# Depthwise convolution taps of a conformer/retention trunk: ScalarE's products summed by accumulating transfers, fewer taps on TensorE, a new order of the planned stage

## The chip, the cores and the metric

The program runs on one core of a Trainium2 chip. The metric is the device time of one execution in microseconds; lower is better. All arithmetic keeps float32 accuracy: a float32 operand of a large matrix product is split into a high part of type float32r and a low part (the rest), and three products (high times high, high times low, low times high) are added in PSUM.

## The reference

Two layers on a sequence of 1024 positions with 1024 channels. Layer 0 mixes with a convolution module, layer 1 with retention; a squared-ReLU MLP follows each. Only layer 0's front part is touched here.

```
cond = silu(c)
for i in range(2):
    mod = cond @ ada_w[i] + ada_b[i]
    sh1, sc1, g1, sh2, sc2, g2 = split(mod, 6)
    h = rmsnorm(x, norm_mix_g[i]) * (1 + sc1) + sh1
    if i == 0:                                   # conformer_conv
        a, g = split(h @ w_pw1 + b_pw1, 2)
        u = a * sigmoid(g)
        u = depthwise_conv(u, w_dw, width=31, causal) + b_dw
        u = layernorm(u) * ln_g + ln_b
        y = silu(u) @ w_pw2 + b_pw2
    else:
        y = retention(h, ...)
    x = x + g1 * y
    h = rmsnorm(x, norm_mlp_g[i]) * (1 + sc2) + sh2
    x = x + g2 * (square(relu(h @ mlp_w1[i])) @ mlp_w2[i])
return rmsnorm(x, final_norm_g)
```

## The kernel before, in words

Channels lie on the 128 partitions (8 tiles, index j or kt), positions along the free dimension in two halves of 512 (t = 0 and t = 1). `layer_conv` builds layer 0's convolution module for both halves and seven eighths of the MLP for half 0 as a list of operations; a planner (`Plan`) then puts them in order. It is a list scheduler: it holds a time for each engine (P TensorE, V VectorE, A ScalarE, G GpSimd, D the SyncE queue of loads), a duration for each operation and a table of priorities `PR`, and picks the operation that can begin first, ties by priority. What it emits is a fixed program order for each engine. On the chip each engine goes through its own list in that order and stops at a semaphore that isn't there yet, so an instruction that waits holds up all behind it on its engine. Everything after `layer_conv` (rest of the MLP, retention, the second MLP, the final norm) is written out by hand and is not touched.

The planned stage does this. SyncE loads half 0 of x, the 16 tiles of `ada` that give shift and scale (sixteen dot products, `moddot`: one pass of a 128x1024 tile times the silu'd condition with a sum, by VectorE alone, or by GpSimd's multiply and ScalarE's sum where `M0POOL`, `M1POOL` or `MODPOOL` say so). From them come `G` and `Sh`, one column of 8 each. Then h0 (8 pieces, split in high and low, tiles hA) is formed, and TensorE begins `pw1`: per channel tile j and half t, 16 steps of three products into two PSUM tiles. The first three channel tiles (`FIRST`) are begun piece by piece as h0 arrives. `pw1` gives u(j,t) (tile x0 or x1, 30 columns of halo ahead of 512).

The 31 taps of u(j,t) are divided by the tables `NPE` (taps on TensorE, a diagonal 128x128 matrix that ScalarE makes, one float32 product per tap, two matmul records each), `NPOOL` (taps whose product ScalarE makes, tile prod, and GpSimd adds to tile cacc) and the rest (VectorE, `acc = u*w + acc` on two PSUM accumulators in turn, so that neighbours do not depend on each other). Two VectorE additions then join cacc and the two accumulators and put the result back into u. When all eight u(j,0) are done, the layer norm (`ln`) gives z0 (tiles hA again), `pw2` multiplies it, a norm (`norm_mlp`) follows, and TensorE runs seven blocks of the MLP on half 0. Meanwhile VectorE, ScalarE and GpSimd do the taps of half 1, whose layer norm gives z1 (tiles hB) for the second `pw2`.

Weights come as 128x1024 float32 tiles (raw, a ring of two); ScalarE copies the high part and VectorE or, where `WPOOL` says so, GpSimd subtracts to get the low part (both into a ring of nine tiles, whl).

In the kernel before, the lines that matter are L263 to L265 (the three products), L625 (low part of a weight tile), L644 (low part of a piece of h0 or h1), L639 (low part of a piece of z), L657 and L654 (moddot on VectorE and on GpSimd), L760 and L763 (G and Sh), L823 (tap on TensorE), L835 (tap on VectorE), L840 and L843 (product on ScalarE and its addition on GpSimd), L845 and L846 (the two joining additions), and L501, a float32 accumulating transfer that GpSimd issues in the second MLP, far behind this stage.

Of the kernel before, what the change touches and what calls it, by code (L numbers as in the profile page):

```python
# [1437 lines left out]
```

## Time and profile before

| | |
|---|---|
| median of three runs | 2687.4 us (2685.89 to 2691.25) |
| the profiled execution's own time | 2684.62 us |
| its span in the trace | 2682.8 us |
| mean granted TensorE clock | 0.983 of full |
| TensorE busy | 2583.2 us (96%) |
| VectorE busy | 1771.8 us (66%) |
| ScalarE busy | 1167.7 us (44%) |
| GpSimd busy | 398.0 us (15%) |

Shares over the whole span mix stages with different limits. The planned stage is the first quarter: its last TensorE work stands at about 721 us, and in it VectorE and GpSimd are far busier than in the mean. TensorE is called busy from the start of the first of several overlapping products to the end of the last; so its rate is read from the distance between starts, not from the length of one record. The same holds for VectorE, whose records overlap by a tenth of a microsecond or so.

### The profile page before, as it was taken

Reading aid. Unit: us, or ns where it says so; the run is one execution under the profiler, and the core shown is the slowest. Engines: PE = TensorE matmul, PEld = TensorE weight load, DVE = VectorE, ACT = ScalarE, POOL = GpSimd, SP = SyncE. Lnnn points to the kernel's source line nnn. Section 1 sums busy time; section 2 is a strip of 40 time slices with the busy share of each in tenths; the row PEclk is TensorE's granted clock in tenths of the full one; section 3 lists DMA queues with packets and bytes.
Section 4 is the critical chain, followed back from the end, with each engine's and each line's share of the span. In section 5 each row is a group of like instructions: output and inputs, shape, how many; then the busy total and the mean of one; then the engine's idle time right before and its main releaser. Section 6 shows DMA issues by size and latency. Waiting matters only on the chain.

```text
span 2682.8 us, 29885 instructions
## 1 busy us (share of the span) xinstructions
PE 2583.2 (96%) x11306; PEld 2089.1 (78%) x11306; DVE 1771.8 (66%) x2513; ACT 1167.7 (44%) x1762; POOL 398.0 (15%) x308
## 2 busy tenths in 40 slices
PE   2999999999999999999999999999999999999996
PEld 1666777888787888788888888888887888888785
DVE  7799999966477445645555665365567677665636
ACT  4666866463222323343433633334545443444323
POOL 3677439100000000000000000000000122111202
PEclk6999999999999999999999999999999999999997
DMA  7622322242376333322233232232332565334712
GB/s 255 204 71 87 114 91 87 88 133 93 119 235 220 101 96 94 116 89 87 71 94 95 72 102 86 80 94 71 95 125 68 114 119 125 75 81 104 196 48 79
DMA packets 95635, 293.26 MB, mean 109 GB/s; under 512 B 10625, under 2 KB 13057, under 8 KB 95362
## 3 DMA queue, kind: packets, MB, share of 16 engines
q1 hardware_dynamic: 78848, 261.37, 30.4%
q0 software_dynamic: 13824, 25.17, 6.2%
q10 hardware_dynamic: 2818, 4.81, 0.5%
q8 instruction: 89, 1.46, 0.2%
q14 instruction: 56, 0.46, 0.1%
HBM read 255.65 MB, written 35.65 MB: 109 GB/s over the span
## 4 chain that ended last, share of the span: by engine, by line
PE 69%; issue 14%; DVE 7%; DMA 4%; POOL 3%; ACT 2%; DVEq 0%; ACTq 0%; POOLq 0%; SPq 0%
PE mm L264 20%; PE mm L263 20%; PE mm L265 20%; DMA araw<-ada 3%; POOL xd L501 3%; PE mm L1064 2%; PE mm L1066 2%; PE mm L1065 2%; DVE acc L835 1%; PE acc L823 1%; DVE araw L324 1%; DVE araw L657 1%; POOL cacc L843 1%; DVE whl L625 1%; PE ax L708 0%
## 5 line engine op out<-in xcount | busy, mean ns | idle before, releaser
L263 PE MATMUL mm<-hA,whl 128*128 128x512 f32 x1200 | 481.0, 401 | 42.3 <-ACT whl L624 39.4
L251 DVE TENSOR_TENSOR whl<-raw,whl 128x1024 fp32r<-128x1024 f32 x240 | 293.3, 1223 | 339.5 <-ACT whl L250 244.3
L250 ACT CAST whl<-raw 128x1024 fp32r<-128x1024 f32 x240 | 251.9, 1050 | 603.9 <-PE mm L264 206.7
L265 PE MATMUL mm<-hA,whl 128*128 128x512 f32 x1200 | 473.9, 395 | 5.7 <-DVE whl L625 3.6
L264 PE MATMUL mm<-hA,whl 128*128 128x512 f32 x1200 | 474.7, 396 | 2.4 <-DVE hA L644 2.2
L263 PE MATMUL mm<-hid,whl 128*128 128x512 f32 (+1 forms) x976 | 375.2, 385 | 4.3 <-ACT hid L286 3.0
L264 PE MATMUL mm<-hid,whl 128*128 128x512 f32 (+1 forms) x976 | 373.5, 384 | 1.2 <-DVE hid L287 1.2
L265 PE MATMUL mm<-hid,whl 128*128 128x512 f32 (+1 forms) x976 | 372.5, 383 | 0.0
L501 POOL DMA_DIRECT2D xd<-ev x72 | 64.2, 913 | 1879.5 <-DVE ev L497 1877.5
L263 PEld LDWEIGHTS mm<-hA,whl 128*128 128x128 f32 x1200 | 226.9, 189 | 99.9 <-ACT whl L624 42.0
L265 PEld LDWEIGHTS mm<-hA,whl 128*128 128x128 f32 x1200 | 226.8, 189 | 60.9 <-DVE whl L625 7.1
L264 PEld LDWEIGHTS mm<-hA,whl 128*128 128x128 f32 x1200 | 226.8, 189 | 58.3 <-issue 4.8
L843 POOL TENSOR_TENSOR cacc<-cacc,prod 128x512 f32<-128x512 f32 x166 | 253.3, 1528 | 112.2 <-ACT prod L840 56.4
L263 PE MATMUL mm<-hB,whl 128*128 128x512 f32 x576 | 229.4, 398 | 0.0
L264 PE MATMUL mm<-hB,whl 128*128 128x512 f32 x576 | 225.0, 391 | 0.0
L265 PE MATMUL mm<-hB,whl 128*128 128x512 f32 x576 | 224.8, 390 | 0.0
L263 PEld LDWEIGHTS mm<-hid,whl 128*128 128x128 f32 x976 | 183.5, 188 | 46.0 <-ACT hid L286 8.6
L264 PEld LDWEIGHTS mm<-hid,whl 128*128 128x128 f32 x976 | 183.8, 188 | 39.4 <-DVE hid L287 3.1
L265 PEld LDWEIGHTS mm<-hid,whl 128*128 128x128 f32 x976 | 183.8, 188 | 35.6 <-issue 0.2
L835 DVE SCALAR_TENSOR_TENSOR acc<-x,vec,acc 128x512 f32<-128x512 f32 x239 | 166.8, 747 | 2.3 <-PE acc L823 1.4
L625 DVE TENSOR_TENSOR whl<-raw,whl 128x1024 fp32r<-128x1024 f32 x92 | 122.7, 1340 | 36.1 <-PE mm L264 10.9
L624 ACT CAST whl<-raw 128x1024 fp32r<-128x1024 f32 x92 | 95.8, 1045 | 101.2 <-DMA raw<-w 42.9
(270 smaller groups left out, 4337.7 us busy)
## 6 DMA issues: line engine op xcount, KB each, us to landing
raw<-w SPq DMA_DIRECT2D x192, 512.0 KB, 3.6
araw<-ada SPq DMA_DIRECT2D x80, 512.0 KB, 4.4
raw<-pw SPq DMA_DIRECT2D x38, 512.0 KB, 4.2
xd<-ev POOLq DMA_DIRECT2D x72, 256.0 KB, 6.2
raw<-rqk SPq DMA_DIRECT2D x32, 512.0 KB, 3.5
raw<-rv SPq DMA_DIRECT2D x32, 512.0 KB, 3.6
raw<-rgate SPq DMA_DIRECT2D x32, 512.0 KB, 3.5
raw<-rout SPq DMA_DIRECT2D x32, 512.0 KB, 3.5
```

Source lines behind the costliest of these rows:

```text
L250: nc.scalar.copy(hi[i], raw[:, i * W : i * W + W])
L251: nc.vector.tensor_tensor(lo[i], raw[:, i * W : i * W + W], hi[i].bitcast(F32), ALU.subtract)
L263: nc.tensor.matmul(out, whi, rhi, start=start, stop=False)
L264: nc.tensor.matmul(out, whi, rlo, start=False, stop=False)
L265: self.last_mm = nc.tensor.matmul(out, wlo, rhi, start=False, stop=stop)
L501: nc.gpsimd.dma_start(xd[n][t], e, accum_op=ALU.add)
L624: op("A", 0.95 / n, pa, lambda h=h, src=src: nc.scalar.copy(E[h], E[raw][:, src]), r=[raw], w=[h], a={h: (tag, kw)})
L625: op(low, dur / n, pa, lambda h=h, l=l, src=src: eng.tensor_tensor(E[l], E[raw][:, src], E[h].bitcast(F32), ALU.subtract), r=[raw, h], w=[ ...
L835: op("V", 0.68, p, lambda s=s, a=a: nc.vector.scalar_tensor_tensor(E[a], sl(s), wv(s), E[a], ALU.mult, ALU.add), r=[u], w=[a])
L843: op("G", 1.28, p, lambda pr=pr: nc.gpsimd.tensor_tensor(E[ca], E[ca], E[pr], ALU.add), r=[pr], w=[ca])
L1064: nc.tensor.matmul(vps[jt], hh[0], wh, start=kt == 0, stop=False)
L1065: nc.tensor.matmul(vps[jt], hh[0], wl, start=False, stop=False)
```

## The change

Taps. `NPE` falls from 53 taps in all to 10, `NPOOL` from 182 to 136, so VectorE's share goes from 261 to 350. GpSimd no longer adds: ScalarE's first product of each of two chains is written to a cacc tile (five in the ring, two before), and each further product is added to it by an accumulating transfer (SBUF to SBUF, 128x512 float32), which GpSimd issues. Each such transfer waits for the one ahead of it in its chain. VectorE's first tap of each accumulator reads cacc, the last tap writes into u, and one joining addition is left of two. The planner gets a field `late`: 5.0 us in which a transfer's result is not there after its issue.

Modulation at the beginning: no moddot of the first sixteen is on GpSimd any more (six were); `G` and `Sh` are formed by ScalarE instead of VectorE. Of the 32 later ones 24 are on GpSimd (10 before). Weights: the low part of every second tile of four of the five groups is made by GpSimd (39 tiles; none before). MLP: for one of four hidden tiles ScalarE does relu and square in PSUM, where VectorE multiplied. All priorities in `PR` are new.

```diff
-X1_AT = 70
-RINGS = dict(raw=2, tmp=4, araw=2, whl=9, hid0=4, sum=2, prod=4, cacc=2, dg=6)
+X1_AT = 80
+RINGS = dict(raw=2, tmp=4, araw=2, whl=9, hid0=4, sum=2, prod=4, cacc=5, dg=2)
...
-NPOOL = ((15, 13, 14, 3, 15, 9, 11, 11), (14, 13, 13, 12, 2, 11, 14, 12))
-NPE = ((6, 8, 6, 6, 1, 0, 6, 10), (6, 0, 0, 0, 0, 1, 3, 0))
+NPOOL = ((0, 7, 9, 6, 12, 6, 12, 8), (10, 23, 2, 5, 12, 11, 4, 9))
+NPE = ((0, 0, 5, 0, 0, 0, 0, 0), (0, 0, 0, 0, 4, 0, 1, 0))
+EVDMA = ()
+RELUA = (0,)
...
-WPOOL = dict(w0=0, w1=8, pw2=0, mlp=0, pw21=0)
-M0POOL = (1, 2, 3)
-M1POOL = (0, 4, 7)
-MODPOOL = dict(m2=2, m3=0, m4=2, m5=3)
+WPOOL = dict(w0=0, w1=2, pw2=2, mlp=2, pw21=2)
+M0POOL = ()
+M1POOL = ()
+MODPOOL = dict(m2=1, m3=0, m4=1, m5=1)
...
+            if o[9]:
+                free["D"] = max(free["D"], t) + 1.7
...
-            op("V", 0.13, ("G", kt), lambda kt=kt: nc.vector.scalar_tensor_tensor(
-                c1("G", kt), c1(("mod", 1), kt), adb[:, kt : kt + 1], self.v("mix_g", kt), ALU.add, ALU.mult),
+            op("A", 0.25, ("G", kt), lambda kt=kt: nc.scalar.activation(
+                c1("G", kt), c1(("mod", 1), kt), AF.Identity, scale=self.v("mix_g", kt), bias=adb[:, kt : kt + 1]),
...
+            fresh = {c for c in range(2) if c or not npe}
+            nca = len(fresh)
+            for i in range(npool):
+                s, c = TAPS - 1 - i, 1 - i % nca
+                ca = k("cacc", c)
+                pr = ca if i < nca else k("prod", s)
...
+                if i >= nca:
+                    op("G", 0.98, p, lambda pr=pr, ca=ca: nc.gpsimd.dma_start(E[ca], E[pr], accum_op=ALU.add), r=[pr], w=[ca], late=5.0)
...
+                if s == 0:
+                    op("V", 0.684, p, lambda a=a: nc.vector.scalar_tensor_tensor(E[u][:, :HALF], sl(0), wv(0), E[a], ALU.mult, ALU.add), r=[a], w=[u])
...
+                elif ca in pl.writer:
+                    inorder("acc", "V", 0.684, p, lambda s=s, a=a, ca=ca: nc.vector.scalar_tensor_tensor(
+                        E[a], sl(s), wv(s), E[ca], ALU.mult, ALU.add), r=[u, "const", ca], w=[a], a={a: ("acc", {})}, lock=True)
...
-                if i:
-                    op("G", 1.28, p, lambda pr=pr: nc.gpsimd.tensor_tensor(E[ca], E[ca], E[pr], ALU.add), r=[pr], w=[ca])
-            a0, a1 = k("acc", 0), k("acc", 1)
-            op("V", 0.62, p, lambda: nc.vector.tensor_tensor(E[ca], E[ca], E[a0], ALU.add), r=[a0], w=[ca])
-            op("V", 0.62, p, lambda: nc.vector.tensor_tensor(E[u][:, :HALF], E[ca], E[a1], ALU.add), r=[ca, a1], w=[u])
+            a = k("acc", 1)
+            op("V", 0.62, p, lambda: nc.vector.tensor_tensor(E[u][:, :HALF], E[u][:, :HALF], E[a], ALU.add), r=[a], w=[u])
...
+                if f in RELUA:
+                    op("A", 0.57, p, lambda ps=ps: nc.scalar.activation(E[ps], E[ps], AF.Relu), w=[ps])
+                    op("A", 0.57, p, lambda ps=ps: nc.scalar.activation(E[ps], E[ps], AF.Square), w=[ps])
```

How the change moves instructions is shown at three places. In these rows the last number of a name tells tiles apart, and "waits" names whose semaphore the instruction waits for (DMAHW: a load, DMASW: a transfer that GpSimd issued, Pool: GpSimd).

First, SyncE's queue at the very beginning, behind the eight loads of x: before,

```order
L651 DMA hid0_41_138<-ada 128x1024 [waits DMAHW2_49]
L307 DMA vec_2_63<-vec 128x336 [waits DMAHW3_49]
L308 DMA ident_6_71<-ident 128x128 [waits DMAHW4_49]
L651 DMA hid0_47_155<-ada 128x1024 [waits DMAHW5_49]
L651 DMA hid0_49_162<-ada 128x1024 [waits DMAHW6_49]
L651 DMA hid0_52_169<-ada 128x1024 [waits DMAHW7_49]
L651 DMA araw_54_175<-ada 128x1024 [waits DMAHW0_49]
L651 DMA hid0_58_186<-ada 128x1024 [waits DMAHW1_49,DVE_49]
```

and now:

```order
L311 DMA vec_2_63<-vec 128x336 [waits DMAHW2_49]
L312 DMA ident_6_71<-ident 128x128 [waits DMAHW3_49]
L624 DMA raw_43_145<-pw1 128x1024 [waits DMAHW4_49,PE_49,Activation_49]
L655 DMA hid0_47_155<-ada 128x1024 [waits DMAHW5_49]
L655 DMA hid0_49_161<-ada 128x1024 [waits DMAHW6_49]
L624 DMA raw_53_169<-pw1 128x1024 [waits DMAHW7_49,DVE_49]
L655 DMA hid0_56_177<-ada 128x1024 [waits DMAHW0_49]
L655 DMA hid0_58_183<-ada 128x1024 [waits DMAHW1_49]
L624 DMA raw_61_191<-pw1 128x1024 [waits DMAHW4_49,DMAHW2_49,DVE_49]
```

The tiles hid0 are the sixteen for shift and scale, araw those of later modulation, raw weights. Ahead of the last hid0 tile there stood five araw tiles and two weight tiles; now there stand three weight tiles and no araw.

Second, GpSimd's list where the taps of half 0 begin: before, the additions for one channel tile, one behind the other,

```order
L843 TENSOR_TENSOR cacc_139_465<-cacc_139_465,prod_164_557 128x512 [waits Activation_49,Pool_49]
L843 TENSOR_TENSOR cacc_139_465<-cacc_139_465,prod_172_593 128x512 [waits Activation_49,Pool_49]
L843 TENSOR_TENSOR cacc_139_465<-cacc_139_465,prod_175_600 128x512 [waits Activation_49,Pool_49]
L843 TENSOR_TENSOR cacc_139_465<-cacc_139_465,prod_180_628 128x512 [waits Activation_49,Pool_49]
L654 TENSOR_TENSOR araw_192_678<-araw_192_678,cond_7_81 128x1024 [waits DMAHW7_49,DVE_49]
```

and now, for channel tiles 1 (cacc_143, cacc_146) and 2 (cacc_161):

```order
L841 DMA cacc_143_496<-prod_153_536 128x512 [waits DMASW0_49,Activation_49]
L841 DMA cacc_146_505<-prod_154_542 128x512 [waits DMASW1_49,Activation_49]
L658 ISA
L658 TENSOR_TENSOR araw_155_557<-araw_155_557,cond_7_81 128x1024 [waits DMAHW6_49,DVE_49]
L841 DMA cacc_161_592<-prod_162_599 128x512 [waits Activation_49]
L841 DMA cacc_143_496<-prod_157_570 128x512 [waits DMASW2_49]
L658 TENSOR_TENSOR araw_164_615<-araw_164_615,cond_7_81 128x1024 [waits DMAHW0_49,DVE_49]
L841 DMA cacc_161_592<-prod_166_629 128x512 [waits DMASW4_49,Activation_49]
L841 DMA cacc_161_592<-prod_168_641 128x512 [waits DMASW6_49,Activation_49]
L841 DMA cacc_161_592<-prod_172_682 128x512 [waits DMASW7_49,Activation_49]
```

Each addition is now a transfer that stands in GpSimd's list and waits for the transfer ahead of it in the same cacc tile. Channel tile 2 has one chain only, with eight transfers.

Third, VectorE's list between two channel tiles of half 0: before,

```order
L835 SCALAR_TENSOR_TENSOR acc_325_1251<-x0_101_317,vec_2_63,acc_325_1251 128x512 [waits DVE_49]
L835 SCALAR_TENSOR_TENSOR acc_301_1127<-x0_101_317,vec_2_63,acc_301_1127 128x512 [waits DVE_49]
L835 SCALAR_TENSOR_TENSOR acc_325_1251<-x0_101_317,vec_2_63,acc_325_1251 128x512 [waits DVE_49]
L845 TENSOR_TENSOR cacc_297_1106<-cacc_297_1106,acc_301_1127 128x512 [waits DVE_49,Pool_49]
L846 TENSOR_TENSOR x0_101_317<-cacc_297_1106,acc_325_1251 128x512 [waits DVE_49]
```

and now:

```order
L851 SCALAR_TENSOR_TENSOR x0_64_200<-x0_64_200,vec_2_63,acc_127_420 128x512 [waits DVE_49]
L863 TENSOR_TENSOR x0_64_200<-x0_64_200,acc_134_453 128x512 [waits DVE_49]
L855 SCALAR_TENSOR_TENSOR acc_187_740<-x0_67_207,vec_2_63,cacc_143_496 128x512 [waits DMASW5_49,Pool_49]
L855 SCALAR_TENSOR_TENSOR acc_189_750<-x0_67_207,vec_2_63,cacc_146_505 128x512 [waits DMASW3_49]
L853 SCALAR_TENSOR_TENSOR acc_187_740<-x0_67_207,vec_2_63,acc_187_740 128x512 [waits DVE_49]
```

The sum of ScalarE's taps was needed at the end of a channel tile; now it is needed at its first VectorE taps, and it comes from a transfer.

## Rows read from the trace of the kernel before

**Rows 1.** Page, part 1: busy time, share of the span and instructions of each engine.

```profile
PE 2583.2 (96%) x11306; PEld 2089.1 (78%) x11306; DVE 1771.8 (66%) x2513; ACT 1167.7 (44%) x1762; POOL 398.0 (15%) x308
```

**Rows 2.** Windows: length, busy us (instructions) by engine, granted clock, DMA share, GB/s.

```profile
0.00:52.70 52.70, 10.03 (x13) 3.22 (x13) 40.33 (x55) 22.59 (x38) 21.64 (x17) 0.63 0.73 256
52.70:75.90 23.20, 17.93 (x49) 11.45 (x49) 20.71 (x27) 9.79 (x15) 6.20 (x5) 0.66 0.68 236
75.90:301.80 225.90, 208.72 (x783) 148.17 (x783) 204.12 (x268) 147.78 (x245) 157.58 (x101) 0.98 0.33 109
301.80:721.50 419.70, 419.45 (x1795) 336.54 (x1796) 339.68 (x454) 225.07 (x314) 110.77 (x71) 1.00 0.33 104
721.50:860.00 138.50, 132.47 (x569) 107.15 (x568) 107.56 (x168) 30.80 (x40) 0.00 (x0) 0.99 0.72 233
```

**Rows 3.** Timeline of TensorE, before h0 and where z0 begins: start, length.

```profile
52.68 0.80 PE L263 MATMUL mm<-hA,whl 128*128 128x512 f32 x1 [36.38 <-ACT whl L624]
...
301.81 0.49 PE L263 MATMUL mm<-hA,whl 128*128 128x512 f32 x1 [0.99 <-ACT hA L638]
```

**Rows 4.** Timeline of VectorE, first 85 us.

```profile
11.30 2.87 DVE L704 TENSOR_TENSOR sum<-tmp,tmp 128x512 f32<-128x512 f32 x1 [0.60 <-PE ax L708]
...
53.80 1.22 DVE L657 SCALAR_TENSOR_TENSOR hid<-hid,cond 128x1024 f32<-128x1024 f32 x1
54.95 0.08 DVE L657 DVE_READ_ACCUMULATOR hid<-hid,cond 128x1 f32 x1
...
72.99 2.89 DVE L644 SCALAR_TENSOR_TENSOR hA<-tmp,Sh,hA 128x512 fp32r<-128x512 f32 x1
```

**Rows 5.** Timeline of GpSimd, first 100 us.

```profile
11.28 2.34 POOL L654 TENSOR_TENSOR hid<-hid,cond 128x1024 f32<-128x1024 f32 x1 [10.83 <-DMA hid<-ada]
```

**Rows 6.** Timeline of SyncE's queue, first 110 us: issues.

```profile
0.74 3.72 SPq L727 DMA_DIRECT2D x<-x  x8
...
50.68 0.38 SPq L651 DMA_DIRECT2D hid<-ada  x1
```

**Rows 7.** Timeline of VectorE, 85 to 302 us.

```profile
217.73 11.94 DVE L835 SCALAR_TENSOR_TENSOR acc<-x,vec,acc 128x512 f32<-128x512 f32 x18
229.58 0.74 DVE L801 SCALAR_TENSOR_TENSOR x<-mm,vec,tmp 128x512 f32<-128x512 f32 x1
...
276.90 4.86 DVE L855 TENSOR_TENSOR x<-x,ax 128x512 f32<-128x512 f32 x8
```

**Rows 8.** Groups of VectorE by form, 0 to 850 us: busy, mean ns | idle before.

```profile
L625 DVE TENSOR_TENSOR whl<-raw,whl 128x1024 fp32r<-128x1024 f32 x92 | 122.7, 1340 | 36.1 <-PE mm L264 10.9 <-issue 9.7 <-ACT whl L624 9.7
...
L657 DVE SCALAR_TENSOR_TENSOR araw<-araw,cond 128x1024 f32<-128x1024 f32 x22 | 34.9, 1598 | 8.0 <-DMA araw<-ada 8.0
...
L760 DVE SCALAR_TENSOR_TENSOR G<-mod,adb,vec 128x1 f32<-128x1 f32 x8 | 7.2, 953 | 0.0
```

**Rows 9.** Groups of GpSimd by form, 0 to 850 us.

```profile
L843 POOL TENSOR_TENSOR cacc<-cacc,prod 128x512 f32<-128x512 f32 x166 | 253.3, 1528 | 112.2 <-ACT prod L840 56.4 <-ACT cacc L840 44.5
L654 POOL TENSOR_TENSOR araw<-araw,cond 128x1024 f32<-128x1024 f32 x10 | 25.8, 2585 | 41.3 <-DMA araw<-ada 28.6 <-DVE acc L835 8.1 <-DVE hB L625 4.6
```

**Rows 10.** Line L501, the accumulating transfers: ns min/median/max of the issue, and landing.

```profile
L501 POOL DMA_DIRECT2D xd<-ev x72: 856/865/1112, 2073.3 to 2524.1; - x72
...
DMA to landing us min/median/max: 3.8/5.7/8.6
```

**Rows 11.** Windows, the stretch of the transfers of L501, columns as in rows 2.

```profile
2073.00:2524.00 451.00, 449.71 (x1960) 367.11 (x1959) 306.87 (x476) 182.24 (x283) 82.63 (x95) 1.00 0.54 111
```

**Rows 12.** Timeline of TensorE around the first taps.

```profile
128.17 0.40 PE L263 MATMUL mm<-hA,whl 128*128 128x512 f32 x1
...
131.43 0.40 PE L265 MATMUL mm<-hA,whl 128*128 128x512 f32 x1
131.67 5.31 PE L823 MATMUL acc<-x,dg 128*128 128x512 f32 x12
136.42 0.80 PE L263 MATMUL mm<-hB,whl 128*128 128x512 f32 x1
```

More of the change, by code (lines that the diff above doesn't have):

```diff
@@ L81, in __init__, with op @@
         self.all_users = {}
-    def op(self, eng, dur, prio, fn, r=(), w=(), a=None, after=(), hold=(), table=None, at=0.0, lock=False):
+    def op(self, eng, dur, prio, fn, r=(), w=(), a=None, after=(), hold=(), table=None, at=0.0, lock=False, late=0.0):
         i = len(self.ops)
@@ L101, in op @@
             self.all_users.setdefault(k, []).append(i)
-        self.ops.append((eng, dur, self.priority(prio, eng), fn, sorted(deps), a or {}, table, at, lock or eng == "G"))
+        self.ops.append((eng, dur, self.priority(prio, eng), fn, sorted(deps), a or {}, table, at, lock or (eng == "G" and not late), late))
         return i
@@ L143, in order @@
                     o = ops[i]
-                    t = max([free[e], o[7], port if o[8] else 0.0] + [end[d] + self.lat(ops[d][0], e) for d in o[4]])
+                    t = max([free[e], o[7], port if o[8] else 0.0] + [end[d] + ops[d][9] + self.lat(ops[d][0], e) for d in o[4]])
                     seen = {}
@@ L191, in order @@
                 if not left[k] and k in home:
-                    freed[home[k]] = max(end[j] for j in self.all_users[k])
+                    freed[home[k]] = max(end[j] + ops[j][9] for j in self.all_users[k])
             for j in outs[i]:
@@ L611, in block @@
         def block(name, ap, p, tag="whl", pa=None, at=0.0, after=(), kind=None):
[L612 removed]
+            low, dur = ("V", 1.135) if not on_pool(count, WPOOL, kind) else ("G", 2.6)
             eng = nc.vector if low == "V" else nc.gpsimd
@@ L816, in taps @@
             k = lambda *a: ("t", j, t) + a
-            nd = TAPS - npool
-            for s in range(npe):
-                dg = k("dg", s)
+            npe = NPE[t][j]
+            for i in range(npe):
+                s, dg, a = TAPS - 1 - npool - i, k("dg", i), k("acc", 0)
                 inorder("dg", "A", 0.293, p, lambda s=s, dg=dg: nc.scalar.activation(E[dg], self.ident, AF.Identity, scale=wv(s)),
                         r=["const"], w=[dg], a={dg: ("dg", dict(cols=P))})
-                first = dict(a={k("acc", 0): ("acc", {})}) if s == 0 else {}
-                inorder("acc" if s == 0 else ("pe", t, j), "P", 0.907, ("dg", 0), lambda s=s, dg=dg: nc.tensor.matmul(
-                    E[k("acc", 0)], E[dg], sl(s), start=s == 0, stop=s == npe - 1), r=[dg, u], w=[k("acc", 0)], **first)
@@ L844, in taps @@
-            a0, a1 = k("acc", 0), k("acc", 1)
-            op("V", 0.62, p, lambda: nc.vector.tensor_tensor(E[ca], E[ca], E[a0], ALU.add), r=[a0], w=[ca])
-            op("V", 0.62, p, lambda: nc.vector.tensor_tensor(E[u][:, :HALF], E[ca], E[a1], ALU.add), r=[ca, a1], w=[u])
+                first = dict(a={a: ("acc", {})}) if i == 0 else {}
+                inorder("acc" if i == 0 else ("pe", t, j), "P", 0.907, ("dg", 0), lambda s=s, dg=dg, a=a, i=i: nc.tensor.matmul(
+                    E[a], E[dg], sl(s), start=i == 0, stop=i == npe - 1), r=[dg, u], w=[a], **first)
```

63 lines of the change are left out of this document (36 added, 27 removed).

## Prediction

> **What bounds the kernel now.** The page's first part calls TensorE busy for 96% of the span [rows 1], which says nothing about one stage, so I cut the span at the places that TensorE's and VectorE's timelines mark. The last piece of h0 is written by the VectorE instruction of 72.99 us, 2.89 us long: h0 is whole at 75.9 us [rows 4]. The first product that reads z0 begins at 301.81 us, where TensorE had waited for the tile [rows 3]. The planned stage ends at about 721.5 us. The windows at these marks [rows 2] show three limits. Up to 75.9 us loads and VectorE set the pace: 256 GB/s in the first window, TensorE mostly idle. From 75.9 to 301.8 us VectorE is busy 204.1 of 225.9 us and TensorE 208.7: both are nearly full. From 301.8 to 721.5 us TensorE is busy 419.45 of 419.70 us, at full clock. Nothing else matters there: what ends the stage is when z0 begins, plus TensorE's list behind it. The part after 721.5 us is the same text in both kernels.
>
> So the sum has two terms: when z0 begins, and how long TensorE's list behind z0 is.
>
> **TensorE's list.** I counted both program orders. Ahead of z0 there are 721 weight products in both, and 43 taps before, 9 now. Behind it there are 1774 weight products in both and 10 taps before, 1 now. Weight products start 0.233 us apart (128.17 to 131.43 us holds 14 steps), a tap takes 4.75/6 = 0.79 us (131.67 to 136.42 us, 12 records for 6 taps) [rows 12]. Behind z0 the change saves 9 x 0.79 = **7.1 us**, on a full engine, so it is real if the products find their operands. Ahead of z0 it frees 34 x 0.79 = 27 us of TensorE, which is worth nothing by itself: the list there is 721 x 0.233 + 9 x 0.79 + 13 sums of a norm, priced like taps, about 185 us, much less than the time z0 will take. The taps move to VectorE, which then decides.
>
> **When h0 is whole.** SyncE's list had 16 ada tiles, 5 later ones, 2 weight tiles, 8 loads of x and two small ones ahead of the last shift tile, 14.4 MB; its issue at 50.68 us [rows 6] and about 5 us to land fit 256 GB/s [rows 2]. Now it has 12.3 MB there: 48 us, and the tile is in at about 49. The sixteen dot products on VectorE follow as tiles land, 1.15 us apart (53.80 to 54.95 us) [rows 4], against about 2 us for a tile to arrive, so they keep up. Up to there VectorE has 25 operations of 512 columns at 0.61 to 0.66, 21 of 1024 at 1.15 and 5 small ones: 41 us, under the 49. Behind the last tile come its dot product, G on ScalarE, two 512-column operations and one weight tile: 3.5 us. h0 is whole at **52.5 us** instead of 75.9. Part of this gain is that GpSimd is silent: before, its multiply at 11.28 us, 2.34 long, held the sum that VectorE began at 11.30 for 2.87 us [rows 4, 5], and G, a single column, took 953 ns in the mean [rows 8]. The G and Sh on ScalarE cost little, since ScalarE was busy 22.6 of 52.7 us [rows 2]; a late one would cost a microsecond or two. Bounds: 49 and 62.
>
> **From h0 to z0 on VectorE.** Rates: 18 taps in 217.73 to 229.58 us are 0.66 each; eight 512-column subtractions in 4.86 us are 0.60 [rows 7]. Before, 131 taps, 34 operations of 1024 columns (18 dot products, 16 low parts), 78 of 512 and a few small ones: 178 us. Now 191 taps, 21 of 1024 columns, 72 of 512: **198 us**. So the taps cost 40, and the dot products and low parts given away return 15.
>
> The stretch took 225.9 us for these 178, a loss of 48. Idle is 225.9 - 204.1 = 22; the other 26 are instructions that last longer than they should, those with two SBUF operands while GpSimd works: low parts 1340 ns in the mean, dot products 1598 [rows 8]. GpSimd was busy 158 of 226 us there [rows 2]. Now the 1.5 us additions [rows 9] are gone from it and about 25 multiplies and low parts at 2.4 to 2.6 remain, some 62 us in 230, 27% in place of 70%. VectorE's instructions with two SBUF operands stay as many (some 65), each meets GpSimd less often but waits longer: 65 x 0.27 x 1.2 = 21 by that, 26 x 62/158 = 10 in proportion; I take 14.
>
> Idle time is the open one: it is where the transfers come in. A chain is serial, since each transfer waits for the one ahead. The trace has no accumulating transfer into SBUF; the nearest row is L501's into DRAM, of the same 256 KB: 0.86 us on GpSimd, landing after 3.8, 5.7 or 8.6 us (least, median, most) [rows 10], with the DMA engines at 54% [rows 11], busier than the 33% of this stretch [rows 2]. I take 6 us a step. Channel tile 2 (one chain, eight transfers) can begin at about 81 us, when its u is there and the dot product ahead of it on GpSimd is done; it ends at 129, and VectorE, by its list, wants it at about 130. Its fourth transfer frees the product buffer on which ScalarE's squares for half 1 queue, so the norm for h1 comes at 112, VectorE there at 109. From then on every pair of chains has 5 to 12 us in hand at 6 us a step. GpSimd's list needs about 20 serial steps for half 0. So idle time is 18 us, less than before (bounds 5 and 40).
>
> The Trainium skill, page "DMA: Bandwidth & Descriptors", section "Anatomy of one DMA", fits a GpSimd-issued transfer as 2.0 us plus its bytes over 436 GB/s. By that a step would be an estimated 2.6 us, a chain of eight 21 us in place of 48, and the idle time would be its lower bound; the row above, twice as long, disagrees with it for accumulating transfers, and I go by the row.
>
> Sum: 52.5 + 198 + 14 + 18 = 282.5 us, against 301.8: **-19.3**.
>
> **Behind z0.** VectorE has 231 us of work up to z1 (232 before), and TensorE's list there is 278 us long (242 before, as the second pw2 is put later), so VectorE has room. New is that GpSimd makes every second weight tile's low part, in a list in which transfers wait. At 6 us a step its low parts are ready about 30 us ahead of need at the start of the MLP, and the 2.6 us each [rows 9] fit in the 11 us that two tiles last. I add 3 us: TensorE starts z0 after idle stretches, and at lower clock (0.66 in the second window [rows 2]) its first products are slower, and some low part may come late (bounds 0 and 20).
>
> **Total**: -19.3 - 7.1 + 3 = -23.4. From the profiled execution's 2684.6 us this is 2661.2; that execution lies 2.8 us under the median, so I predict **2664 us**.
>
> **Rivals.** 0.2% is 5.4 us, about what a measurement can tell.
>
> Slower: the chain is slow. At 8.6 us a step, the largest of the row, half 0's 20 serial steps take 172 us; with 70 for their start and 25 of dot products that don't hide, the last channel tile's sums are in at 267 us, where VectorE wants them at 222. The 40 us behind them and 8 of waits in the norm put z0 at 315 (+13). GpSimd then reaches the weights' low parts some 60 to 95 us later than at 6 us, and TensorE stands 15 to 25 us for them. With -7 this is +21 to +31, 2710 us. It decides from about 7.7 us a step. For it: the landing spreads to 8.6, and loads are dense at 60 to 110 us. Against it: the median. Chance 0.15. The same page (section "SWDGE vs HWDGE vs iDMA") says that GpSimd writes such a transfer's descriptors into SBUF, state from which VectorE can lock it out; by it the issue itself would be stretched and the step with it. L501 stood beside a VectorE busy 307 of 451 us [rows 11] and its issue never took over 1.11 us [rows 10], so the trace speaks against more than 0.25 us a step.
>
> No change: VectorE loses as much as before, 48 to 52 us, because GpSimd's longer multiplies meet it at the norm of half 1 and TensorE, idle until h1, gives the last u late. Then z0 is at 299 to 303 us: -3 + 3 - 7, about 2680 to 2683. For it: 60 more taps on the engine that sets z0. Against: GpSimd's busy share falls by more than half. Chance 0.11.
>
> More: chains are as quick as the lower end, h0 at 50, loss 15. z0 at 263, total -46, 2641 us. Chance 0.17.
>
> The forecast, loss of 25 to 42 us: 2650 to 2678, chance 0.57.
>
> **How the numbers follow.** Faster by over 0.2% are the forecast and the better case, 0.74; within 0.2%, 0.11; slower, 0.15. The range of 8 in 10 takes in the forecast, half of the better case, the unchanged case and the edge of the slow one: 2646 to 2692.
>
> **What would show it.** In the trace after: no GpSimd multiply before 70 us, and the eighth L648 into hA ends at 49 to 56 us; the landing of L841's transfers at 4 to 7 us; the first product on z0 at 270 to 292; from there to the end of the stage 410 to 416 us with TensorE idle under 5; VectorE idle ahead of L855 under 15 us in all. The prediction is wrong if L841 lands later than 7.5 us, if TensorE waits for L629's low parts from GpSimd, or if h0 is late because the ada tiles wait in their ring of four.

## The result, and the profile after

The changed kernel takes **2655.6 us** (median of 4 runs, 2652.95 to 2659.43) where the kernel before takes 2686.95: ratio 0.9884, 95% interval 0.987 to 0.9898, 31 us less. The prediction was 2664 us, with 2646 to 2692 as its range. The profiled execution took 2654.15 us, its span (first to last instruction) is 2652.4.

New line numbers: L263 to L265 are L267 to L269, the low parts are L629, moddot is L661 and L658, ScalarE's product L838, the transfer L841, VectorE's taps L853 and, where a chain's sum comes in, L855.

Windows of the kernel after, up to h0, from h0 to z0 and from z0 to the mark behind the stage; columns as in [rows 2]. The last row is that of the kernel before from z0 to a mark that both traces show, the first product behind the stage that waits for `x` (L920, now L947).

```profile
0.00:51.04 51.04, 27.70 (x55) 14.29 (x56) 41.36 (x69) 26.48 (x45) 1.19 (x12) 0.70 0.84 289
51.04:272.94 221.90, 184.54 (x724) 138.40 (x722) 210.40 (x297) 138.02 (x219) 117.18 (x84) 0.92 0.79 200
272.94:693.23 420.29, 416.58 (x1787) 336.56 (x1787) 323.13 (x435) 212.27 (x295) 132.90 (x88) 0.99 0.54 135
```

```profile
301.81:725.60 423.79, 421.75 (x1804) 338.10 (x1804) 341.97 (x457) 226.11 (x315) 110.77 (x71) 1.00 0.33 103
```

Timelines of VectorE and TensorE, kernel after: the last piece of h0, the first product on z0 with the wait ahead of it, the 22nd, and the mark behind the stage.

```profile
50.28 0.74 DVE L648 SCALAR_TENSOR_TENSOR hA<-tmp,Sh,hA 128x512 fp32r<-128x512 f32 x1
```

```profile
272.94 0.80 PE L267 MATMUL mm<-hA,whl 128*128 128x512 f32 x1 [6.63 <-ACT hA L642]
...
280.99 0.39 PE L267 MATMUL mm<-hA,whl 128*128 128x512 f32 x1
...
693.23 0.50 PE L267 MATMUL mm<-hA,whl 128*128 128x512 f32 x1 [1.92 <-DVE x L947]
```

h0 is whole at 51.0 us (75.9 before), z0 begins at 272.9 (301.8 in [rows 3]): 28.9 us earlier. The stretch behind it is 3.5 us shorter, the rest of the program 2.0 us longer (1959.2 against 1957.2 us): together the 30.4 us by which the span is shorter. The 2.0 us can't be put down to the change: behind the mark both kernels are the same text, and it took 1958.4 to 1964.0 us in six of the runs below.

The transfers, kernel after: the issues, who waited for them, and their landing.

```profile
L841 POOL DMA_DIRECT2D cacc<-prod x109: 813/862/1576, 68.3 to 456.4; - x109
...
  POOL cacc L841: 67.1, 23
  ACT prod L838: 21.6, 21
  DVE acc L855: 1.0, 1
...
DMA to landing us min/median/max: 3.2/5.0/8.4
```

GpSimd waited 67 us in its list for landings; VectorE waited 1.0 us in all. VectorE's groups from h0 to z0, kernel after (columns as in rows 8):

```profile
L629 DVE TENSOR_TENSOR whl<-raw,whl 128x1024 fp32r<-128x1024 f32 x14 | 16.9, 1217 | 0.3 <-ACT whl L628 0.3
L855 DVE SCALAR_TENSOR_TENSOR acc<-x,vec,cacc 128x512 f32<-128x512 f32 x15 | 13.0, 894 | 1.0 <-DMA cacc<-prod 1.0
L806 DVE SCALAR_TENSOR_TENSOR x<-mm,vec,tmp 128x512 f32<-128x512 f32 x15 | 11.2, 747 | 5.2 <-ACT tmp L797 5.0
L648 DVE SCALAR_TENSOR_TENSOR hB<-tmp,Sh,hB 128x512 fp32r<-128x512 f32 x8 | 9.7, 1248 | 0.0
...
L708 DVE TENSOR_TENSOR sum<-sum,x 128x512 f32<-128x512 f32 x6 | 8.2, 1363 | 0.2
```

A low part of a weight tile takes 1217 ns in the mean here, where those of the same stretch took 1664 before; the 1340 of [rows 8] are a mean up to 850 us. The kernel before, 75.9 to 301.8 us:

```profile
L625 DVE TENSOR_TENSOR whl<-raw,whl 128x1024 fp32r<-128x1024 f32 x16 | 26.4, 1664 | 1.4 <-ACT prod L840 0.8 <-ACT whl L624 0.6
```

What is still stretched are instructions with two SBUF operands that GpSimd's multiplies happen to meet: L648 at 1248 ns, L708 at 1363 (748 and 690 with the multiplies cut to one column, below). The largest idle time is that ahead of L806, 5.0 of 11.5 us. L806 waits for the sigmoid, L797, and ScalarE stood ahead of that for TensorE's product, from h0 to z0:

```profile
  PE mm L269: 12.7, 8
```

### The profile page after: what moved, and what is told of

Same layout as the page of the kernel before. It is cut to its first block, busy times and chain, and to the rows that moved or that the text cites. A ratio compares the mean times of both kernels' runs of the same rounds, so it can differ in the third digit from the quotient of the medians.

```text
span 2652.4 us, 29653 instructions
## 1 busy us (share of the span) xinstructions
PE 2554.1 (96%) x11220; PEld 2077.1 (78%) x11220; DVE 1739.2 (66%) x2508; ACT 1137.9 (43%) x1708; POOL 352.7 (13%) x298
## 4 chain that ended last, share of the span: by engine, by line
PE 65%; issue 18%; DMA 6%; DVE 5%; POOL 3%; ACT 3%; DVEq 0%; POOLq 0%; ACTq 0%; SPq 0%
PE mm L268 19%; PE mm L267 19%; PE mm L269 19%; DMA araw<-ada 3%; POOL xd L505 3%; PE mm L1092 2%; PE mm L1091 2%; PE mm L1093 2%; DMA cacc<-prod 2%; DVE araw L328 1%; DVE acc L853 1%; PE ax L712 1%; POOL araw L658 0%; DVE hid L661 0%; ACT prod L838 0%
## 5 line engine op out<-in xcount | busy, mean ns | idle before, releaser
L255 DVE TENSOR_TENSOR whl<-raw,whl 128x1024 fp32r<-128x1024 f32 x240 | 293.1, 1222 | 340.3 <-ACT whl L254 245.2
L267 PE MATMUL mm<-hA,whl 128*128 128x512 f32 x1200 | 479.3, 399 | 23.7 <-ACT hA L646 15.1
L269 PE MATMUL mm<-hA,whl 128*128 128x512 f32 x1200 | 474.1, 395 | 2.4 <-DVE whl L255 2.0
L267 PE MATMUL mm<-hid,whl 128*128 128x512 f32 (+1 forms) x976 | 375.5, 385 | 5.2 <-ACT hid L290 3.5
L269 PE MATMUL mm<-hid,whl 128*128 128x512 f32 (+1 forms) x976 | 372.4, 383 | 0.0
L267 PEld LDWEIGHTS mm<-hA,whl 128*128 128x128 f32 x1200 | 227.2, 189 | 80.7 <-ACT hA L646 17.3
L269 PEld LDWEIGHTS mm<-hA,whl 128*128 128x128 f32 x1200 | 227.3, 189 | 54.6 <-DVE whl L255 2.9
L267 PE MATMUL mm<-hB,whl 128*128 128x512 f32 x576 | 226.9, 394 | 6.2 <-ACT hB L646 6.2
L269 PE MATMUL mm<-hB,whl 128*128 128x512 f32 x576 | 225.7, 392 | 0.0
L267 PEld LDWEIGHTS mm<-hid,whl 128*128 128x128 f32 x976 | 183.3, 188 | 46.7 <-ACT hid L290 8.8
L269 PEld LDWEIGHTS mm<-hid,whl 128*128 128x128 f32 x976 | 183.8, 188 | 35.5 <-issue 0.2
L853 DVE SCALAR_TENSOR_TENSOR acc<-x,vec,acc 128x512 f32<-128x512 f32 x305 | 210.6, 748 | 0.9
L267 PEld LDWEIGHTS mm<-hB,whl 128*128 128x128 f32 x576 | 109.1, 189 | 31.1 <-ACT hB L646 7.0
L268 PEld LDWEIGHTS mm<-hB,whl 128*128 128x128 f32 x576 | 108.9, 189 | 28.2 <-DVE hB L648 4.2
```

What stands on the lines that cost most here:

```text
L255: nc.vector.tensor_tensor(lo[i], raw[:, i * W : i * W + W], hi[i].bitcast(F32), ALU.subtract)
L267: nc.tensor.matmul(out, whi, rhi, start=start, stop=False)
L268: nc.tensor.matmul(out, whi, rlo, start=False, stop=False)
L269: self.last_mm = nc.tensor.matmul(out, wlo, rhi, start=False, stop=stop)
L853: op("V", 0.684, p, lambda s=s, a=a: nc.vector.scalar_tensor_tensor(E[a], sl(s), wv(s), E[a], ALU.mult, ALU.add), r=[u], w=[a])
```

## The experiments

Times are medians; "the kernel before" in each comparison is its own runs on the same chip, 2685.7 to 2687.7 us. Of each edit the lines or the call that differ are shown, with "..." where something is left out. In the first two runs the planner made a new order for the changed tables, so each is its edit together with a new order; where "order kept" is said, every engine's list is that of the kernel after.

**Taps alone, in the kernel before.**

```diff
-NPE = ((6, 8, 6, 6, 1, 0, 6, 10), (6, 0, 0, 0, 0, 1, 3, 0))
+NPE = ((0, 0, 5, 0, 0, 0, 0, 0), (0, 0, 0, 0, 4, 0, 1, 0))
```

> The kernel before, with nothing changed but the table of TensorE's taps (53 in all to 10; ahead of z0 43 to 9); VectorE takes the 43, additions stay on GpSimd. Theory 1 (VectorE sets when z0 begins): 34 more taps at 0.66 us ahead of z0 move it from 301.8 us to 318 to 326; TensorE's list behind z0 is 7 us shorter; sum +9 to +17 us, 2696 to 2704 us. Theory 2 (TensorE, busy 208.7 of 225.9 us there, sets it): 34 fewer taps at 0.79 us move z0 to 275 to 285, sum -24 to -34 us, 2653 to 2663 us.

Measured 2709.98 us, 1.0081 (1.0066 to 1.0096) of before. Timeline of TensorE:

```profile
298.13 2.08 PE L708 MATMUL ax<-sum,ones 128*128 128x512 f32 x2 [30.50 <-DVE sum L704]
...
316.34 0.80 PE L263 MATMUL mm<-hA,whl 128*128 128x512 f32 x1 [6.21 <-ACT hA L638]
```

z0 is 14.5 us later (316.3 us, just under theory 1's range) while TensorE stands 30.5 us for VectorE: theory 1, and theory 2 falls. The time is 6 us above theory 1's range, because behind z0 the span is 9.4 us longer instead of 7 shorter: among TensorE's waits there are 7.1 and 3.0 us for the pieces of the norm ahead of the MLP.

**The start alone, in the kernel before.**

```diff
-M0POOL = (1, 2, 3)
-M1POOL = (0, 4, 7)
+M0POOL = ()
+M1POOL = ()
```

> The kernel before, with the first sixteen dot products all on VectorE (six were split between GpSimd and ScalarE); G and Sh stay on VectorE, and the bytes ahead of the last shift tile stay near 14.3 MB. Theory 1 (GpSimd's multiplies stretch VectorE and stand in the chain): h0 whole at 60 to 68 us instead of 75.9, z0 7 to 13 us earlier, 2674 to 2681 us. Theory 2 (the bytes loaded ahead, and VectorE's own work of 7 us more, set h0): h0 whole at 72 to 80 us, time within 5 us of 2687.

Measured 2701.5 us, 1.005 (1.0038 to 1.0063). The last pieces of h0, and windows from h0 to z0 and from z0 to the mark:

```profile
58.03 2.72 DVE L644 SCALAR_TENSOR_TENSOR hA<-tmp,Sh,hA 128x512 fp32r<-128x512 f32 x4
```

```profile
60.75:299.78 239.03, 217.38 (x821) 154.10 (x819) 214.41 (x276) 151.06 (x251) 155.55 (x101) 0.98 0.33 110
```

```profile
299.78:738.41 438.63, 428.19 (x1804) 341.67 (x1804) 346.18 (x455) 225.90 (x313) 111.60 (x71) 0.98 0.32 100
```

Neither theory: h0 is whole at 60.75 us as theory 1 said, but z0 gains only 2.0 us, since 38 more of TensorE's records and 10 us more of VectorE's work stand between h0 and z0. Behind z0 the same 1804 records of TensorE take 438.6 us in place of 423.8: the planner, with the old priorities, put them in another order, and TensorE is idle for 10 us where it was for 2, and busy 6 us longer, at a granted clock of 0.98 in place of 1.00.

**Only the priorities.** The kernel after with the table `PR` of the kernel before; no instruction is added or taken away. For G and Sh on ScalarE, which the old table doesn't know, the new table's entry stands.

```diff
-PR = dict(h0=dict(A=350, V=206), ...
+PR = {'h0': {'A': 504, 'V': 930}, ...
```

> The kernel after with the priority table of the kernel before (the one missing entry, for G and Sh on ScalarE, from the new table); all instructions the same, only their order differs. Theory 1 (the new order is a part of the gain: with the old table both changes of the kernel before alone lost some 15 us behind z0, the norm ahead of the MLP being no longer covered): z0 at 285 to 300 us, 2675 to 2705 us. Theory 2 (the order is incidental, the gain lies in which engine does what): within 6 us of 2656.

Measured 2688.06 us, 1.0008 (0.9999 to 1.0018): the whole gain is gone. Window from h0 to z0:

```profile
57.91:302.91 245.00, 198.28 (x754) 146.94 (x752) 221.09 (x304) 135.42 (x213) 108.00 (x89) 0.91 0.74 183
```

Theory 1 by its time, but the loss is not where that theory put it: z0 comes at 302.9 us, above its 285 to 300, and behind z0 nothing is lost (420.9 us). Of the 30.0 us at z0, 6.9 stand ahead of h0 and 23.1 in the window above. The weights for TensorE's first products are loaded from 42 us on, behind the ada tiles (in the kernel after from 8 us, between them), so 30 more of TensorE's records lie behind h0; VectorE is busy 10.7 us longer and idle 12 us longer. With both experiments before it: taps alone and start alone lose, and all instructions together gain nothing, as long as the order is made by the old table; with the new one they give 31 us. So the 31 us are shown for instructions and order together, and not for the order alone: the new table on the kernel before was not tried.

**Additions on GpSimd again.** Order kept.

```diff
-nc.gpsimd.dma_start(E[ca], E[pr], accum_op=ALU.add)
+nc.gpsimd.tensor_tensor(E[ca], E[ca], E[pr], ALU.add)
```

> The kernel after with its program order kept word for word, but each of the 109 accumulating transfers is again an addition on GpSimd (128x512, some 1.53 us). Theory 1 (the transfers help by taking GpSimd's work off the side of VectorE): about 56 additions ahead of z0, 86 us of two-operand work on GpSimd; at the 26 us that VectorE lost beside 158 us of it before, 14 us are lost anew, and z0 comes 9 to 15 us later: 2664 to 2671 us. Theory 2 (how the products are summed does not matter, the gain is h0 and the dot products): 2651 to 2659 us. Theory 3 (the serial transfers cost, and an addition is shorter than a landing): z0 some microseconds earlier, 2644 to 2651 us.

Measured 2677.63 us, 0.9961 (0.9948 to 0.9974), 22 us above the kernel after. Window from h0 to z0, and VectorE's groups in it:

```profile
51.30:290.40 239.10, 185.48 (x721) 138.66 (x719) 235.17 (x298) 136.45 (x218) 152.54 (x86) 0.90 0.38 125
```

```profile
L855 DVE SCALAR_TENSOR_TENSOR acc<-x,vec,cacc 128x512 f32<-128x512 f32 x15 | 22.8, 1550 | 0.0
L629 DVE TENSOR_TENSOR whl<-raw,whl 128x1024 fp32r<-128x1024 f32 x14 | 22.3, 1607 | 0.0
L708 DVE TENSOR_TENSOR sum<-sum,x 128x512 f32<-128x512 f32 x6 | 11.8, 1971 | 0.2
```

Theory 1, with a larger price: z0 is 17.5 us later, where 9 to 15 were expected. VectorE idles 7.6 us less (it waits for no landing, and 0.9 us in place of 5.0 ahead of L806) and is busy 24.8 us longer, on the instructions with two SBUF operands alone. The list was made for transfers; one planned for additions was not tried.

**GpSimd's multiplies cut to one column.**

```diff
-nc.gpsimd.tensor_tensor(E[raw], E[raw], self.cond, ALU.mult)
+nc.gpsimd.tensor_tensor(E[raw][:, :1], E[raw][:, :1], self.cond[:, :1], ALU.mult)
```

> The kernel after, its order kept, but GpSimd's 24 multiplies for the later modulation work on one column in place of 1024 (so this modulation is left out of the result); they last some 2.7 us each in the kernel after, 64 of GpSimd's 125 us ahead of z0. Theory 1 (what VectorE still loses, 12.4 us of longer instructions, it loses beside GpSimd's long two-operand work): VectorE's busy time from h0 to z0 falls from 210.4 to 199 to 203 us, z0 at 260 to 266, 2643 to 2650 us. Theory 2 (VectorE's instructions wait beside the issuing of the transfers as well, 51 us of GpSimd there): busy time stays at 206 us or more, z0 at 268 to 273, 2651 to 2656 us.

Measured 2645.5 us, 0.9847 (0.9825 to 0.9868), 10 us under the kernel after. Window from h0 to z0; groups of VectorE, and one of GpSimd:

```profile
51.06:261.01 209.95, 181.63 (x721) 137.12 (x720) 199.63 (x297) 137.49 (x219) 64.51 (x84) 0.94 0.84 211
```

```profile
L855 DVE SCALAR_TENSOR_TENSOR acc<-x,vec,cacc 128x512 f32<-128x512 f32 x15 | 10.8, 753 | 0.0
L708 DVE TENSOR_TENSOR sum<-sum,x 128x512 f32<-128x512 f32 x6 | 4.1, 690 | 0.2
```

```profile
L841 POOL DMA_DIRECT2D cacc<-prod x56 | 49.8, 928 | 117.0 <-DMA cacc<-prod 53.0 <-ACT prod L838 48.6 <-ACT tmp L797 6.5
```

Theory 1: 10.8 us of VectorE's time in the kernel after are waits beside the multiplies. The 50 us in which GpSimd issues transfers cost VectorE nothing that the rows show: its means of 753 and 690 ns are close to the shortest such instructions of the kernel after, 746 and 691.

**The multiplies of the start on GpSimd again.** Order kept.

```diff
+                    if (kind, kt) not in ((0, 1), (0, 2), (0, 3), (1, 0), (1, 4), (1, 7)):
+                        return nc.vector.scalar_tensor_tensor(E[raw], E[raw], 1.0, self.cond, ALU.mult, ALU.mult, accum_out=col())
+                    nc.gpsimd.tensor_tensor(E[raw], E[raw], self.cond, ALU.mult)
+                    nc.scalar.activation(E[raw], E[raw], AF.Copy, accum_out=col())
```

> The kernel after, its order kept, but six of the first sixteen dot products are made by GpSimd's multiply and ScalarE's sum, the same six as in the kernel before. Theory 1 (GpSimd at the start stretches VectorE's operations and stands in the chain to h0): h0 whole at 55 to 62 us in place of 51.0, and z0 later by 4 to 10 us, 2660 to 2667 us. Theory 2 (the loads set h0, and 6.9 us less on VectorE make up for it): h0 whole at 49 to 53 us, 2652 to 2658 us.

Measured 2664.86 us, 0.9916 (0.9903 to 0.9929), 9 us above the kernel after. The last piece of h0, and the first product on z0:

```profile
58.38 0.74 DVE L648 SCALAR_TENSOR_TENSOR hA<-tmp,Sh,hA 128x512 fp32r<-128x512 f32 x1
```

```profile
284.19 0.80 PE L267 MATMUL mm<-hA,whl 128*128 128x512 f32 x1 [6.65 <-ACT hA L642]
```

h0 is whole at 59.1 us. Theory 1: in this order the 8 us there are worth 11 at z0, where 4 to 10 were expected; in the kernel before 15 us at h0 had brought 2.

**Low parts of weights on VectorE.** Order kept.

```diff
-            eng = nc.vector if low == "V" else nc.gpsimd
+            eng = nc.vector
```

> The kernel after, its order kept, with the 39 low parts of weights that GpSimd makes given to VectorE at the same places of the list. Theory 1 (they are worth little: VectorE has 100 us to spare behind z0, and four lie ahead of it): 4 x 1.14 = 4.6 us more on VectorE ahead of z0, less up to 4 us of waits beside GpSimd, so 2654 to 2661 us. Theory 2 (GpSimd's list, in which the low parts stand behind transfers that wait, holds TensorE up): 2645 to 2652 us. Theory 3 (they are a main part of the gain, as VectorE with 35 more of them is late for TensorE or for z1): 2665 us and more.

Measured 2666.16 us, 0.9934 (0.992 to 0.9947), 10.6 us above the kernel after. Window from z0 to the mark, and a wait of ScalarE in it, in this run and in the kernel after:

```profile
275.94:703.60 427.66, 418.97 (x1787) 335.75 (x1787) 345.87 (x470) 211.77 (x295) 43.72 (x51) 0.99 0.52 131
```

```profile
ACT hid L930 <- DVE mm L928: 27.9, 15, 4.7
```

```profile
ACT hid L930 <- DVE mm L928: 12.1, 12, 2.1
```

z0 is 3.0 us later, and the stretch behind it 7.4 us longer, though VectorE is busy only 81% of it: that is theory 3, and theory 1 falls. VectorE is late with its products for the hidden tiles of the MLP (L928, for which ScalarE waits 27.9 us in place of 12.1), and TensorE waits 3.6 us for these tiles, where it waited for none. The other 3.8 us of the stretch are not put down to anything here.

**A third of the transfers twice, all of them twice.**

```diff
-nc.gpsimd.dma_start(E[ca], E[pr], accum_op=ALU.add)
+[nc.gpsimd.dma_start(E[ca], E[pr], accum_op=ALU.add) for _ in range(2 if i % 3 == 2 else 1)][-1]
```

> The kernel after with about one in three of its accumulating transfers issued twice (each such product is counted twice in the sum), so that a mean step of a chain takes a third longer, some 7.8 us in place of 5.9; the order is kept. All transfers twice took z0 from 272.9 to 449.6 us. Theory 1 (the prediction's: 7.7 us a step is the point at which the gain over before is gone): z0 at 295 to 310 us, 2680 to 2700 us. Theory 2 (GpSimd's list has slack, 31 us of its waits ahead of z0 are for landings and VectorE waited 1 us, so that a third more is hidden): z0 at 273 to 283 us, 2656 to 2667 us. Theory 3 (GpSimd waits in order, a third of the loss of all twice): z0 at 320 to 340 us, over 2740 us.

> The kernel after with every accumulating transfer issued twice, one behind the other (each such product is counted twice in the sum), so that a step of a chain takes some 11 us in place of 5.9. Theory 1 (the prediction's: the chains have 5 to 12 us in hand and decide from 7.7 us a step; z0 at 143 us plus 20 serial steps): z0 at 340 to 365 us, and GpSimd's low parts late behind it, 2725 to 2765 us. Theory 2 (the chains have much slack, since VectorE waited 1.0 us for them in all): z0 at 275 to 295 us, 2656 to 2680 us.

Measured 2775.93 us (1.0335, 1.0321 to 1.035) and 3013.05 us (1.1214, 1.1195 to 1.1232); z0 at 341.2 and 449.6 us. Of the third twice: the issues, GpSimd's idle time ahead of them for a landing, ScalarE's wait for a landing, and whom TensorE waited for from 51 to 812 us.

```profile
L841 POOL DMA_DIRECT2D cacc<-prod x150: 852/877/1842, 68.6 to 579.8; - x150
...
  DMA cacc<-prod: 222.3, 57
...
  ACT prod L838: 112.5, 44
```

```profile
PE mm L269 <- DVE whl L629: 22.1, 5, 10.4
PE mm L269 <- POOL whl L629: 21.3, 5, 5.7
```

Theory 3 of the first, and both theories of the second fall short. 41 transfers more are 155 us more of waits on GpSimd (222.3 against 67.1), 3.8 us for each, where the median landing in that run is 4.3 us: little of it is hidden. ScalarE, whose products then find no free tile, stands 112 us, and its sigmoids and high parts, which are in the same list, with it.

**Products that nobody reads, to keep TensorE's clock up.** Order kept; 14 and 5 products on a free PSUM tile ahead of z0, first at a wrong place, then behind the last pw1 product.

```diff
+for _ in range(n):
+    nc.tensor.matmul(wm, self.ones, self.cond[:, :HALF], start=True, stop=True)
```

> The kernel after, its order kept, with 14 products that nobody reads put behind TensorE's last pw1 product ahead of z0 and 5 behind the last sum of the layer norm, where TensorE stands idle for 16.7 and 6.6 us and its clock falls. Theory 1 (the low clock at z0 costs about 3 us, the 15 first products taking 6.4 us in place of 3.4, and 1 us in the norm's sums): 2651 to 2653 us. Theory 2 (the clock at z0 is worth nothing, because something else ends the stage): 2655 to 2657 us. Theory 3 (the added products hold up the norm's sums or z0): 2657 us and more.

> As the run before with products that nobody reads, which put them 21 us too early (ahead of two channel tiles of pw1, and so held z0 up by 12 us); now the 14 stand behind the last pw1 product ahead of z0, where TensorE is idle for 16.7 us, and 5 behind the last sum of the layer norm. Theory 1 (the low clock at z0 costs about 3 us, the 15 first products taking 6.4 us in place of 3.4, and 1 us in the sums): 2651 to 2653 us, z0 at 272 and the stage behind it 417 us long. Theory 2 (the clock at z0 is worth nothing): 2655 to 2657 us.

Measured 2666.44 us (0.9924, 0.9911 to 0.9937) and 2657.37 us (0.9886, 0.987 to 0.9901; 2651.73 to 2665.56). At the wrong place, timelines of TensorE and VectorE:

```profile
214.04 12.18 PE L698 MATMUL mm<-cond,ones 128*128 128x512 f32 x28
```

```profile
237.87 0.75 DVE L820 SCALAR_TENSOR_TENSOR x<-mm,vec,tmp 128x512 f32<-128x512 f32 x1 [7.99 <-ACT tmp L811]
```

12 us more of TensorE's work at 214 us made z0 12.2 us later: theory 3, and more than was asked, for it shows that TensorE has no slack there. At the right place, at 236.8 us, the median is not told from the kernel after. The first product on z0 in the second run:

```profile
281.67 0.79 PE L267 MATMUL mm<-hA,whl 128*128 128x512 f32 x1 [2.37 <-ACT hA L642]
```

What the clock costs is not settled by these runs: the 5 products did not hold it. They ran at a granted clock of 1.00, TensorE then stood 2.37 us, and from 281.67 to 284.00 us the granted clock was 0.50, that is 1.2 GHz (0.79 us for the first product, 0.40 at full clock). The profiled execution of the second was its slowest, 2665.56 us; in it VectorE's low parts before z0 took 1555 ns in the mean against 1217, with the same list, and z0 came 8.7 us later than in the kernel after. So VectorE and GpSimd can meet differently with the same list; whether chance or the added products did it here is not shown.

**Another table.** New priorities, x of half 1 later, 14 products of half 1 from ScalarE to VectorE and four taps of TensorE too.

```diff
-NPOOL = (..., (10, 23, 2, 5, 12, 11, 4, 9))
+NPOOL = (..., (0, 20, 8, 3, 12, 9, 2, 8))
```

> The kernel after with other numbers in its tables: priorities, x of half 1 loaded from 85 in place of 80, and the taps of half 1 divided anew (ScalarE's products of half 1 from 76 to 62, TensorE's from 5 to 1). Theory 1 (the order decides, as the run with the old priorities says, and 14 fewer transfers give GpSimd room; the table is not at its best): 2640 to 2652 us. Theory 2 (the table is as good as the list scheduler's picture of the chip goes, and what it can't see, waits beside GpSimd and late transfers, takes a gain back): 2652 to 2665 us. Theory 3 (14 taps more on VectorE behind z0, or later low parts, cost): over 2665 us.

Measured 2667.55 us, 0.9922 (0.9909 to 0.9936), 12 us above the kernel after: theory 3 by its time. z0 begins at 272.6 us, as in the kernel after; from there to the end the span is 13.5 us longer, with one wait of 6.8 us for a hidden tile right behind the stage, at 750 us. Which of its many edits costs this was not tried apart. No version here beats the kernel after with the whole work done.

## Why the prediction was right, and where it was off

The prediction's sum was -23.4 us; the span came out 30.4 shorter. The terms account for the difference: h0 came 1.5 us earlier than predicted, collisions cost 1.6 less, idle time 6.5 less, the stretch behind z0 gained 0.6 less, and the 2.0 us behind the mark were not in the sum. Of the signs that it named, h0 (51.0 us), the first multiply on GpSimd (80.3 us), the landing (5.0 us), z0 (272.9 us) and VectorE's wait ahead of L855 (1.0 us) came as it said; the stretch behind z0, 3.5 us shorter than its 419.7, lies at the upper edge of its 410 to 416.

**When h0 is whole.** 52.5 us predicted, 51.0 measured. That GpSimd's multiplies were part of the old 75.9 holds: put back, they cost 8 us.

**VectorE's work of 198 us.** Right: with hardly anything of GpSimd in its way VectorE is busy 199.6 us in this stretch.

**Collisions of 14 us.** 210.4 - 198 = 12.4 measured, 10.8 of it removed with the multiplies. The prediction had two estimates, 21 and 10, and took a number between them, so that it came so close is in part luck. The additions on GpSimd would have cost 24.8 us more.

**Idle time of 18 us: the term that was mis-sized.** It is 221.9 - 210.4 = 11.5 us. The step took the chains for its main part, at 6 us a transfer; the landing is 5.0 us, and VectorE waited 1.0 us for chains. Of what idles, 5.0 us are the wait for the next u.

The estimate of 2.6 us that the prediction worked out from the Trainium skill, page "DMA: Bandwidth & Descriptors", section "Anatomy of one DMA", lies under even the quickest landing of 3.2 us. The row of L501 was the better guide.

**Behind z0.** -7.1 + 3 predicted, -3.5 measured. The clock's part is in the rows of z0's first 22 products, after and before:

```profile
272.94:280.99 8.05, 8.05 (x22) 5.67 (x22) 8.05 (x14) 7.86 (x13) 1.72 (x2) 0.61 0.85 221
```

```profile
301.81:307.29 5.48, 5.25 (x21) 4.06 (x22) 5.48 (x8) 5.35 (x9) 0.00 (x0) 1.00 0.59 190
```

They take 2.6 us longer, at a granted clock of 0.61 in the mean in place of 1.00; TensorE had stood 6.63 us just ahead of them, and 0.99 us in the kernel before. TensorE waits for no low part of GpSimd's there.

**"Worth nothing by itself", of the 27 us that TensorE is freed of.** The reason given, that a list of 185 us ahead of z0 leaves TensorE room, does not hold. VectorE does decide (34 taps given to it cost 14.5 us at z0), but up to the last u TensorE's list decides when VectorE may go on: in the kernel after, 12 us more there are 12 us at z0. What the freed 27 us brought was not measured apart. That the sum came out all the same, since it was read from the new lists, in which TensorE starts early, is argued and not shown.

**What the prediction never weighed** is the order itself. It read VectorE's work and SyncE's queue from the new lists, so the order was in its numbers; that the same instructions in the old order gain nothing (2688 us) it did not see.

**The slow chain** was a true rival with too mild a price. Its mechanism is seen in both runs with doubled transfers, TensorE waiting for GpSimd's low parts among it (21.3 and 97.4 us). GpSimd's list is one queue, and each wait in it holds up all chains: a third more steps costs 120 us where the rival had its point of decision, so its 20 serial steps look too few; the count itself was not measured. The other way to a slow chain, that the issue itself is stretched beside VectorE, is small here: the issue took 862 ns in the median and 1576 at most.

**The better case** (loss of 15, 2641 us) is what the multiplies stood against: with them cut, the loss is 261.0 - 51.06 - 198 = 12 us, and the time 2645.5.

## What to carry to other kernels

Judge a reordering by the work that stands ahead of and behind each mark on every engine, and time the same instructions in the old order before you credit the instructions. Moving additions from GpSimd to transfers pays where VectorE has two-operand work, since issuing a transfer leaves VectorE alone and an addition does not; but a serial chain of transfers belongs in a list only while each landing is covered by other work of that list. An engine with spare time in the sum can still have none up to one tile that another engine waits for.

## What was not expected of the hardware

An accumulating transfer of 256 KB from SBUF to SBUF lands after 3.2, 5.0 or 8.4 us (least, median, most), and after 3.9 us in the median of the run with all of them twice, where GpSimd's issues stopped 115 times for a landing. That is no slower than L501's into DRAM [rows 10].

VectorE's waits beside GpSimd fall on few instructions, and those wait long. Its sums (L708) took 690 ns in the mean with the multiplies cut, 1363 with them and 1971 with the additions as well, while taps, whose other operand lies in PSUM, stayed at 744 to 748 ns in all three. Two sums of the kernel after, and GpSimd's multiply beside the second:

```profile
149.01 0.69 DVE L708 TENSOR_TENSOR sum<-sum,x 128x512 f32<-128x512 f32 x1
...
189.69 2.22 DVE L708 TENSOR_TENSOR sum<-sum,x 128x512 f32<-128x512 f32 x1
```

```profile
188.97 2.40 POOL L658 TENSOR_TENSOR araw<-araw,cond 128x1024 f32<-128x1024 f32 x1 [0.81 <-DMA araw<-ada]
```

The multiply ends at 191.37 us, the sum 0.54 us behind it. With the additions on GpSimd, one sum waited through all that GpSimd did without a pause:

```profile
226.61 6.36 DVE L708 TENSOR_TENSOR sum<-sum,x 128x512 f32<-128x512 f32 x1
```

```profile
224.99 2.57 POOL L841 TENSOR_TENSOR cacc<-cacc,prod 128x512 f32<-128x512 f32 x2
227.49 2.43 POOL L658 TENSOR_TENSOR araw<-araw,cond 128x1024 f32<-128x1024 f32 x1
229.84 2.58 POOL L841 TENSOR_TENSOR cacc<-cacc,prod 128x512 f32<-128x512 f32 x2
```

GpSimd's last one ends at 232.42 us, the sum at 232.97. So an instruction of VectorE with two SBUF operands did not get its turn between GpSimd's instructions there: a list on GpSimd without pauses can hold it up for several of them.

The Trainium skill, page "SBUF — State Buffer", section "SBUF: two separate sides", says that an instruction of VectorE with two SBUF inputs and one of GpSimd that reads SBUF exclude each other for a whole instruction. The sum at 189.69 us agrees; the one at 226.61 us took 5.67 us beyond the 0.69 that it takes alone, longer than any one of GpSimd's instructions beside it. That the transfers' issues held nobody up is shown by the run with the multiplies cut.
